# First feed-forward product as seven half-size products, its weight sums made in DRAM during the mixer

## The chip, the core and the metric

One core of a Trainium2 chip runs one launch of the kernel. The metric is the device time of that launch in microseconds; smaller is better. Engines work side by side, each in the order of its own instruction list: TensorE (PE) multiplies, VectorE (DVE) and ScalarE (ACT) do elementwise work, GpSimd (POOL) does some elementwise work and issues transfers, SyncE (SP) only issues transfers.

## The reference

One residual layer on x of 512 tokens and 1024 channels, in float32:

```python
D_MODEL = 1024; SEQ = 512; D_FF = 4 * D_MODEL
...
for l in range(DEPTH):
    h = rms_norm(x, norm_mix_pre[l])
...
    x = x + rms_norm(merged @ w_out[l], norm_mix_post[l])
    h = rms_norm(x, norm_ffn_pre[l])
    f = jnp.square(jax.nn.relu(h @ w_ff1[l])) @ w_ff2[l]
    x = x + rms_norm(f, norm_ffn_post[l])
```

The lines left out are the mixer: one input projection of h, cut into the parts of three branches (gated DeltaNet, stick-breaking attention, short gated convolution), whose outputs sigmoid gates merge. The part that changes is `h @ w_ff1`: 512 x 1024 by 1024 x 4096, and what feeds and follows it.

## The kernel before

All large products run on PE in float32r, each as three passes: both operands are split into a high and a low part, and high x high, high x low and low x high are summed in one bank (`mm3`, one instruction a pass through `mm`, L179). A weight tile (128 x 1024, 512 KB) is loaded by SP into `raw` (two buffers, `wload` L140), ACT casts it to the high part (L143), DVE subtracts to get the low part (L144); `hl` has three buffers. Every product is fed this way, so a weight tile costs one load, one ACT and one DVE instruction.

The Tile scheduler fixes each engine's order when the kernel is built; priorities (`early`, `urgent`) and the order of the code decide it. On the chip an engine takes its list strictly in order.

Stages: input projection and mixer (the `proj` calls, with the branches woven between them by lanes of generators), gates, out-projection (bank `po`), and for each of four blocks of 128 tokens a post-norm residual (`out_norm`: x1, then h2), transposes on PE (`out_transpose`, L898) and a split into `h2h` and `h2l`. Then ff1: 32 output tiles of 128 features, each 8 k-tiles x 3 passes of 512 columns (tokens); the first three tiles (`lead`) are done as two halves of 256 columns, the first half from token blocks 0 and 1 while blocks 2 and 3 are still being normalized. `ff1_act` takes relu on ACT (L942) and squares on DVE (L947) into the tiles `aT[i]`, i the half of the tokens.

ff2 is already done by seven products of half size in place of eight (Strassen's scheme in Winograd's form): the matrices are cut 2 x 2, and sums of blocks enter as operands. The sums of weight blocks it needs, S5, S6 and S1, are made in DRAM by `presum`: SP copies one block from DRAM to DRAM (L172), later POOL issues a transfer that adds the second block to it (L168). There are 24 such jobs; before, four are issued in the gate stage and twenty in ff1. POOL's elementwise work in the mixer is small but on the branches' path: `sv` and `DT` of each DeltaNet head (L456, L460), the masks of attention scores `z` (L651), the scratch transfers of a triangular inverse (`scr`, `tc`, L497 to L519) and the memset of `TT` (L525).

Of the kernel before, what the change touches and what calls it, by code (L numbers as in the profile page):

```python
# [62 lines left out]
def trunk_kernel(ctx, tc, keys, xT, xtok, wst, wab, cst, vec, alog, dtb, wpost, wffn, wfpost, out):  # L63
# [92 lines left out]
    for u in range(8):
        jobs.append((S5[u], ("ff2", 1, 8 + u), ("ff2", 1, u)))
    for u in range(8):
        jobs.append((S6[u], ("ff2", 0, u), ("ff2", 1, u)))
    for u in range(8):  # L160
        jobs.append((S1[u], S5[u], ("ff2", 0, u)))
# [762 lines left out]
    def ff1_mm(w, ps, ts_):  # L924
        wh = w[:, 0, :].rearrange("p (k c) -> p k c", k=KT)
        wl = w[:, 1, :].rearrange("p (k c) -> p k c", k=KT)
        for k in range(KT):
            mm3(ps[:, ts_], wh[:, k, :], wl[:, k, :], h2h[:, k, ts_], h2l[:, k, ts_], k == 0, k == KT - 1)

# [6 lines left out]
    def ff1_act(f, ps):  # L936
        u = f // 2
        if f % 2 == 0:
            for i in range(2):
                aT[i].append(g2("aT", F32, (P, 2, 256)))  # L940
        r = sm.tile([P, 512], F32, tag="r", bufs=2, name=nm("r"))
        x = nc.scalar.activation(r, ps, AF.Relu)  # L942
        if ready:
            dep(x, after[0])
        for i in range(2):
            c = slice(i * 256, i * 256 + 256)
            x = nc.vector.tensor_tensor(aT[i][u][:, f % 2, :], r[:, c], ps[:, c], ALU.mult)  # L947
            if ready:
                dep(x, after[1])
        if f % 2 == 1 and u >= 8:  # L950
            X.append(g2("X", F32, (P, 2, 256)))
            nc.vector.tensor_tensor(flat(X[-1]), flat(aT[0][u]), flat(aT[0][u - 8]), ALU.subtract)
            W.append(aT[0][u])
            nc.vector.tensor_tensor(flat(W[-1]), flat(W[-1]), flat(aT[1][u]), ALU.subtract)
# [2 lines left out]
    for i, (w, ps) in enumerate(lead):
        ff1_mm(w, ps, slice(0, 256))
        if i > 0:
            out_transpose(i + 1, h2s[i + 1])  # L960
    for f, (w, ps) in enumerate(lead):
        ff1_mm(w, ps, slice(256, 512))
        ff1_act(f, ps)
    NJ, NR = 4, 3
# [8 lines left out]
    def right(src, plus=None):  # L973
        if turn["r"] < NR:
            raw = ring("r", raws)
        else:
            if turn["r"] == NR:
                raws.clear()
                for _ in range(2):
                    t = hp.tile([P, 4, 1024], F32, tag="h16", name=nm("ch"))  # L980
                    raws.extend([(slice(0, 1024), t[:, i, :])] for i in range(4))
            raw = ring("r", raws)
# [31 lines left out]
    for f in range(3, 30):  # L1014
        if f >= 6:
            presum()
        w = wnext("ff1", f)
        ps = mbank()
        ff1_mm(w, ps, slice(0, 512))
        ff1_act(f, ps)  # L1020
    late = [(wnext("ff1", 30), mbank())]
    ff1_mm(*late[0], slice(0, 512))
    late.append((wnext("ff1", 31), mbank()))
    ready.append(unit(A10, block(0, 0), 0))
    ff1_act(30, late[0][1])
    ff1_mm(*late[1], slice(0, 512))
    ready.append(unit(A10, block(0, 0), 1))
    ff1_act(31, late[1][1])
# [168 lines left out]
```

## Time and profile before

| what | value |
|---|---|
| time of the kernel before, median of 3 runs | 908.04 us (906.22 to 908.98) |
| profiled execution, its own time | 908.15 us |
| its span in the trace | 906.4 us |
| PE busy | 884.8 us (98%) |
| DVE, ACT, POOL busy | 588.5, 451.8, 106.4 us |
| mean granted clock of PE | 0.995 |
| ff1, the piece at 512 columns | 587.11 to 744.90 us |

The profile is of one execution. The span runs from the first to the last instruction of the core; the time of the execution is a little longer. Busy time of an engine is a sum over the whole span: a stage may be bound by another engine than the mean suggests.

### The profile page before, as it was taken

What the parts mean: (1) busy time and instruction counts of PE and PEld (TensorE: products, weight loads), DVE (VectorE), ACT (ScalarE), POOL (GpSimd) and SP (SyncE); (2) the same over time, 40 slices, a digit from 0 to 9 for tenths busy, and PEclk for the clock granted to TensorE, in tenths of its full rate; (3) what the DMA queues carried; (4) which work ended last, traced back from release to release, by engine and by line L of the source; (5) the groups of instructions that cost most, each with busy time, mean ns of one, the idle gap of its engine ahead of it and who ended that gap; (6) DMA issues with size and microseconds to landing.
All of it is one profiled execution on the core that took longest, in us unless ns stands there. A gap on an engine that the chain in (4) does not pass through costs nothing.

```text
span 906.4 us, 11714 instructions
## 1 busy us (share of the span) xinstructions
PE 884.8 (98%) x4204; PEld 735.0 (81%) x4204; DVE 588.5 (65%) x1022; ACT 451.8 (50%) x823; POOL 106.4 (12%) x165
## 2 busy tenths in 40 slices
PE   7999999999999999999999999999999999999996
PEld 6778888877877888888888878988888888888884
DVE  4786678987778659655565546533334459878885
ACT  7455875657787732232344333422223337566562
POOL 1003222010112120200000111011111000000020
PEclk9999999999999999999999999999999999999998
DMA  9322223231213134524243552299999339565792
GB/s 316 119 71 93 73 74 122 70 106 51 68 57 104 51 125 116 163 94 116 70 151 119 180 190 94 86 298 284 278 286 274 125 117 364 189 198 193 202 270 86
DMA packets 41627, 136.97 MB, mean 151 GB/s; under 512 B 5456, under 2 KB 5456, under 8 KB 41184
## 3 DMA queue, kind: packets, MB, share of 16 engines
q1 hardware_dynamic: 34176, 111.50, 35.1%
q0 software_dynamic: 7248, 24.68, 13.1%
q8 instruction: 33, 0.54, 0.2%
q14 instruction: 26, 0.21, 0.1%
q10 hardware_dynamic: 144, 0.04, 0.0%
HBM read 131.48 MB, written 29.88 MB: 178 GB/s over the span
## 4 chain that ended last, share of the span: by engine, by line
PE 81%; DVE 10%; ACT 3%; issue 3%; DMA 2%; POOL 0%; DVEq 0%; SPq 0%; POOLq 0%; ACTq 0%
PE mm L179 51%; PE Q L179 5%; PE R L179 5%; PE S L179 5%; PE po L179 3%; PE psv L179 3%; PE V L179 2%; DVE hl L144 2%; DVE c L682 2%; PE p L179 2%; DMA raw<-wst 1%; DVE z L683 1%; DVE XX L513 1%; PE pg L179 1%; DVE XX L507 1%
## 5 line engine op out<-in xcount | busy, mean ns | idle before, releaser
L179 PE MATMUL mm<-hh,hl 128*128 128x512 f32 x928 | 305.8, 397 | 0.9 <-ACT ct L729 0.9
L143 ACT CAST hl<-raw 128x1024 fp32r<-128x1024 f32 x116 | 111.6, 962 | 222.3 <-PE mm L179 154.3
L144 DVE TENSOR_TENSOR hl<-raw,hl 128x1024 fp32r<-128x1024 f32 x116 | 129.0, 1112 | 142.5 <-ACT hl L143 142.2
L179 PEld LDWEIGHTS mm<-hh,hl 128*128 128x128 f32 x928 | 173.9, 188 | 35.7 <-ACT ct L729 1.3
L179 PE MATMUL mm<-hl,hl 128*128 128x512 f32 x464 | 181.2, 390 | 0.0
L179 PE MATMUL mm<-h2h,hl 128*128 128x512 f32 (+1 forms) x528 | 155.2, 377 | 0.4 <-ACT h2h L187 0.2
L179 PEld LDWEIGHTS mm<-h2h,hl 128*128 128x128 f32 x528 | 97.2, 188 | 19.0 <-ACT h2h L187 0.8
L179 PEld LDWEIGHTS mm<-hl,hl 128*128 128x128 f32 x464 | 87.4, 188 | 16.1
L179 PE MATMUL mm<-h2l,hl 128*128 128x512 f32 (+1 forms) x264 | 99.5, 377 | 0.1
L997 DVE TENSOR_TENSOR hl<-ch,hl 128x1024 fp32r<-128x1024 f32 x53 | 64.7, 1223 | 6.2 <-ACT hl L996 6.1
L179 PEld LDWEIGHTS mm<-h2l,hl 128*128 128x128 f32 x264 | 49.7, 188 | 9.3 <-DVE h2l L188 0.3
L996 ACT CAST hl<-ch 128x1024 fp32r<-128x1024 f32 x53 | 55.3, 1046 | 0.0
L179 PE MATMUL po<-wo,mg 128*128 128x512 f32 x192 | 45.3, 391 | 0.5 <-ACT mg L187 0.5
L179 PEld LDWEIGHTS po<-wo,mg 128*128 128x128 f32 x192 | 35.8, 188 | 8.5 <-ACT mg L187 1.0
L179 PE MATMUL Q<-hl,ahi 128*128 128x512 f32 x128 | 39.7, 391 | 0.0
L179 PE MATMUL R<-hl,ahi 128*128 128x512 f32 x128 | 39.4, 389 | 0.0
L179 PE MATMUL S<-hl,ahi 128*128 128x512 f32 x128 | 39.4, 389 | 0.0
L168 POOL DMA_DIRECT2D S<-wst x24 | 19.9, 830 | 152.0 <-DMA S<-wst 115.1
L682 DVE TENSOR_TENSOR_SCAN c<-c,w 128x512 f32<-128x512 f32 (+3 forms) x32 | 25.5, 816 | 14.9 <-ACT w L106 14.9
L187 ACT CAST ahi<-aT 128x512 fp32r<-128x512 f32 x32 | 19.8, 622 | 28.7 <-PE Q L179 12.1
L179 PEld LDWEIGHTS Q<-hl,ahi 128*128 128x128 f32 x128 | 23.9, 188 | 5.7 <-ACT hl L996 0.4
L947 DVE TENSOR_TENSOR aT<-r,mm 128x256 f32<-128x256 f32 x62 | 23.1, 415 | 7.7 <-ACT r L942 7.7
(287 smaller groups left out, 1442.0 us busy)
## 6 DMA issues: line engine op xcount, KB each, us to landing
raw<-wst SPq DMA_DIRECT2D x92, 512.0 KB, 3.3
ch<-S SPq DMA_DIRECT2D x32, 512.0 KB, 3.3
raw<-wst SPq DMA_DIRECT2D x48, 256.0 KB, 3.3
S<-wst POOLq DMA_DIRECT2D x24, 512.0 KB, 9.1
ch<-wst SPq DMA_DIRECT2D x21, 512.0 KB, 5.1
S<-wst SPq DMA_DIRECT2D x16, 512.0 KB, 8.1
S<-S SPq DMA_DIRECT2D x8, 512.0 KB, 9.7
ch<-wst POOLq DMA_DIRECT2D x8, 512.0 KB, 8.4
```

The costliest lines, as they stand in the source:

```text
L143: nc.scalar.copy(hl[:, 0, :], raw)
L144: nc.vector.tensor_tensor(hl[:, 1, :], raw, rf(hl[:, 0, :]), ALU.subtract)
L168: nc.gpsimd.dma_start(t, wsrc(1024, *key), accum_op=ALU.add, max_dma_last_dim=4096)
L179: return nc.tensor.matmul(o, l, r, start=start, stop=stop, skip_group_check=more)
L187: nc.scalar.copy(hi, src)
L507: nc.vector.tensor_tensor(tmp[:, :, :w], X[:, :, j].unsqueeze(2).to_broadcast([P, 8, w]), L[:, j, j + 1:].unsqueeze(1).to_broadcast([P, 8, ...
L513: nc.vector.tensor_tensor(X[:, :, j + 1:], X[:, :, j + 1:], tmp[:, :, :w], ALU.subtract)
L682: nc.vector.tensor_tensor_scan(back, back, w[j][:, ks][:, ::-1], 0.0, ALU.add, ALU.add)
L683: nc.vector.tensor_tensor(z[j][:, :n], z[j][:, :n], c[j][:, :n], ALU.subtract)
L947: x = nc.vector.tensor_tensor(aT[i][u][:, f % 2, :], r[:, c], ps[:, c], ALU.mult)
L996: after[0] = nc.scalar.copy(hl[0][:, c], r)
L997: after[1] = nc.vector.tensor_tensor(hl[1][:, c], r, rf(hl[0][:, c]), ALU.subtract)
```

## The change

ff1 becomes seven products too. The token half i and the feature half n give blocks: A of the activations (A00, A01, A10, A11: token half, channel half) and four blocks of w_ff1. With X, Y, Z, W as sums of activation blocks and F1, F5, F6, F7 as sums of weight blocks, M1 to M7 are seven products of 256 tokens x 512 channels x 2048 features in place of eight. Each product is cut into eight steps u of 256 features: two output tiles of 128 features lie side by side in one bank of 512 columns, and each takes 4 k-tiles x 3 passes = 12 matmuls of 256 columns, so 24 for a step. M5 is summed into M3's bank, M4 into M2's and M7 into M1's. `step` recombines the banks on DVE and takes relu and square; M3's bank is copied out by ACT. `combine` makes X, Y, Z and W on DVE from float32 copies `F` of the transposes, made by ACT, and splits each. F1, F5, F6 and F7 are 32 more `presum` jobs; these are issued from the third `proj` call on, `quiet` keeping some stretches of the triangular inverse free, and from every fourth product of ff1. The store of x1 goes from SP's to POOL's queue. Weights of ff1 go through a ring of five load buffers (the two `raw`, and three pairs of `rw`).

```diff
+    F5, F6, F1, F7 = (sums("F", n) for n in (5, 6, 1, 7))
+    plan(F5, f1(1, 1), f1(0, 1))
+    plan(F6, f1(0, 0), f1(0, 1))
+    plan(F1, F5, f1(0, 0))
+    plan(F7, F1, f1(1, 0))
...
     def presum():
+        if quiet[0]:
+            return
         while added and (len(added) > LAG or not jobs):
...
     def proj(c0, x=False):
+        calls[0] += 1
+        if calls[0] > 2:
+            presum()
         w = wnext("in", c0)
...
-            nc.sync.dma_start(x1d[b, hf], x1[hf])
+            nc.gpsimd.dma_start(x1d[b, hf], x1[hf])
...
-            split(h2h[:, q * 4:q * 4 + 4, bs], h2l[:, q * 4:q * 4 + 4, bs], p3)
+            if b % 2 == 0:
+                FB[i, q] = [g2("F", F32, (P, 2, 256)) for _ in range(2)]
+            for g in range(2):
+                nc.scalar.copy(FB[i, q][g][:, :, ts_], p3[:, 2 * g:2 * g + 2, :])
...
+        if i == 0:
+            combine(("A", 0, 0), FB[0, 0])
+            FB["X"] = [g2("X", F32, (P, 2, 256)) for _ in range(2)]
+            combine("X", FB["X"], FB[0, 1], FB[0, 0])
+        else:
+            combine(("A", 1, 0), FB[1, 0])
+            combine(("A", 1, 1), FB[1, 1])
+            combine("Y", FB["X"], FB[1, 1], FB["X"])
+            combine("Z", FB[1, 0], FB[1, 0], FB["X"])
+            combine("W", FB[0, 1], FB[0, 1], FB[1, 1])
+
+    def combine(name, o, a=None, b=None):
+        if name not in op:
+            op[name] = [[g2("op", F32R, (P, 2, 256)) for _ in range(2)] for _ in range(2)]
+        for g in range(2):
+            if a is not None:
+                nc.vector.tensor_tensor(o[g], a[g], b[g], ALU.subtract)
+            split(op[name][0][g], op[name][1][g], o[g])
...
-    lead = [(wnext("ff1", f), mbank()) for f in range(2)] + [(wnext("ff1", 2), bank("f1"))]
...
+    left = {"M1": "Y", "M2": ("A", 1, 0), "M3": "X", "M4": ("A", 1, 1), "M5": ("A", 0, 0), "M6": "Z", "M7": "W"}
...
+    def ff1_product(m, ps, u, first):
+        done[0] += 1
+        if done[0] > 5 and done[0] % 4 == 0:
             presum()
...
+        hi, lo = op[left[m]]
+        for j in range(2):
+            o = ps[:, j * 256:j * 256 + 256]
+            for k in range(4):
+                c = slice(k * 256 + j * P, k * 256 + j * P + P)
+                xh_, xl_ = hi[k // 2][:, k % 2, :], lo[k // 2][:, k % 2, :]
+                mm(o, w[0][:, c], xh_, first and j == 0 and k == 0, False, True)
+                mm(o, w[0][:, c], xl_, False, False, True)
+                mm(o, w[1][:, c], xh_, False, k == 3, True)
...
+        if m == "M3":
+            pb["R", u] = mbank()
+            ff1_product(m, pb["R", u], u, True)
+            nc.scalar.copy(new(1, 8 + u), pb["R", u])
...
+        elif m == "M5":
+            ff1_product(m, pb["R", u], u, False)
+            relu2(new(0, 8 + u), pb["R", u])
...
+    quiet[0] = False
+    step("M3", 0)
+    step("M3", 1)
+    out_transpose(2, h2s[2])
+    step("M5", 0)
+    out_transpose(3, h2s[3])
+    step("M5", 1)
+    for m in ("M2", "M4", "M1", "M6", "M7"):
+        step(m, 0)
+        if m in ("M2", "M4"):
+            step(m, 1)
+    for m in ("M1", "M6", "M7"):
+        step(m, 1)
+    for u in range(2, 8):
+        for m in ("M3", "M2", "M5", "M4", "M1", "M6", "M7"):
+            step(m, u)
```

How the order of instructions moves, at three places. A row is a line, an operation, its output and inputs with buffer numbers, and the output's shape; x23 is 23 such in a row.

The first place is PE behind the out-projection, at the start of ff1. Before, `pt` are transposes of blocks, `mm` and `f` the banks of the lead's tiles, whose halves begin between the transposes of block 2:

```order
L898 MATMUL pt_5188<-cs,h_953_5080 128x128 x4
L898 MATMUL pt_5195<-cs,h_954_5081 128x128 x4
L898 MATMUL pt_5268<-cs,h_960_5125 128x128 x3
L179 MATMUL mm_5207<-h2h,hl_5203 128x256
L179 MATMUL mm_5213<-h2h,hl_5209 128x256
L898 MATMUL pt_5268<-cs,h_960_5125 128x128
L898 MATMUL pt_5275<-cs,h_961_5126 128x128 x4
L179 MATMUL f_981_5219<-h2h,hl_5215 128x256
```

In the changed kernel `pt_5312` and `pt_5319` are of block 1, the next two of block 2 and the last two of block 3; `h_921` holds the split X and A00, `h_922` the split A10 and A11, `mm_5346` and `mm_5378` are the banks of M3 and M5 for u = 0 and 1, `Q` those of M2 and M4:

```order
L928 MATMUL pt_5312<-cs,h_961_5200 128x128 x4
L928 MATMUL pt_5319<-cs,h_962_5201 128x128 x4
L928 MATMUL pt_5410<-cs,h_968_5245 128x128 x4
L928 MATMUL pt_5419<-cs,h_969_5246 128x128 x4
L928 MATMUL pt_5463<-cs,h_981_5308 128x128 x4
L928 MATMUL pt_5470<-cs,h_982_5309 128x128 x4
L197 MATMUL mm_5346<-h_921_4973,hl_5349 128x256
L197 MATMUL mm_5378<-h_921_4973,hl_5381 128x256
L197 MATMUL mm_5346<-h_921_4973,hl_5349 128x256 x23
L197 MATMUL mm_5378<-h_921_4973,hl_5381 128x256 x23
L197 MATMUL mm_5346<-h_921_4973,hl_5430 128x256 x24
L197 MATMUL mm_5378<-h_921_4973,hl_5517 128x256 x24
```

The first product of ff1 now stands behind the transposes of the last block, where it stood between those of block 2.

The second place is ACT at the same time. Before, the casts of the last transposes (`h2h`), the weight casts and the relus of the lead follow each other:

```order
L861 ACTIVATE r_5175,st<-x_946_5035 128x512
L861 ACTIVATE r_5179,st<-x_947_5037 128x512
L187 CAST h2h<-pt_5306 128x4x128
L187 CAST h2h<-pt_5313 128x4x128
L143 CAST hl_5423<-raw_5422 128x1024
L942 ACTIVATE r_5346<-mm_5207 128x512
L143 CAST hl_5457<-raw_5456 128x1024
```

In the changed kernel `aT` are the copies of M3's banks, `F` those of the transposes of blocks 2 and 3, `hl_5430` the weights of M5 u = 0:

```order
L1088 COPY aT_5376<-mm_5346 128x512
L1088 COPY aT_5408<-mm_5378 128x512
L933 COPY F_5415<-pt_5410 128x2x128
L933 COPY F_5416<-pt_5410 128x2x128
L933 COPY F_5424<-pt_5419 128x2x128
L933 COPY F_5425<-pt_5419 128x2x128
L933 COPY F_5415<-pt_5463 128x2x128
L933 COPY F_5416<-pt_5463 128x2x128
L933 COPY F_5424<-pt_5470 128x2x128
L933 COPY F_5425<-pt_5470 128x2x128
L205 CAST h_922_4974<-F_5415 128x512
L205 CAST h_922_4974<-F_5416 128x512
```

and right behind them, with the relu of M5 u = 0 (`r_5460`), the casts of Y, Z and W (`op`) and the weights of M5 u = 1 (`hl_5517`):

```order
L205 CAST h_922_4974<-F_5424 128x512
L1025 CAST hl_5430<-rw_5100 128x512
L1025 CAST hl_5430<-rw_5101 128x512
L205 CAST h_922_4974<-F_5425 128x512
L1072 ACTIVATE r_5460<-mm_5346 128x512
L205 CAST op_5485<-X_5330 128x512
L205 CAST op_5486<-X_5331 128x512
L205 CAST op_5495<-F_5415 128x512
L205 CAST op_5496<-F_5416 128x512
L205 CAST op_5505<-F_5263 128x512
L205 CAST op_5506<-F_5264 128x512
L1025 CAST hl_5517<-rw_5102 128x512
```

The weights of M5 now stand behind the copies of M3's banks, the copies of the transposes and the operand casts.

The third place is POOL in the mixer, between the transfers of two DeltaNet heads (`scr`). Before:

```order
L497 DMA scr_1295<-AD_1009 128x4x32
L456 TENSOR_TENSOR sv_1106<-ske_1105,half 128x4
L460 TENSOR_TENSOR DT_765<-DT_765,wd_1107 128x512
L651 AFFINE_SELECT z_1190<-z_1190 128x128
L651 AFFINE_SELECT z_1191<-z_1191 128x256
L651 AFFINE_SELECT z_1192<-z_1192 128x128
```

In the changed kernel, where `F` are the weight sums in DRAM:

```order
L519 DMA scr_1350<-AD_1058 128x4x32
L186 DMA F_85<-wst 128x1024
L477 TENSOR_TENSOR sv_1157<-ske_1156,half 128x4
L481 TENSOR_TENSOR DT_806<-DT_806,wd_1158 128x512
L186 DMA F_86<-wst 128x1024
L676 AFFINE_SELECT z_1243<-z_1243 128x128
L676 AFFINE_SELECT z_1244<-z_1244 128x256
L676 AFFINE_SELECT z_1245<-z_1245 128x128
```

Two accumulating transfers have come in, one ahead of the head's `sv` and one ahead of the masks.

## Rows read from the trace of the kernel before

**Rows 1.** The page, busy time, share of the span and instructions of each engine.

```profile
PE 884.8 (98%) x4204; PEld 735.0 (81%) x4204; DVE 588.5 (65%) x1022; ACT 451.8 (50%) x823; POOL 106.4 (12%) x165
```

**Rows 2.** Chain of waits, out-projection to ff1: start us, us, what.

```profile
560.33 5.51 PE po L179 x24
...
584.35 2.76 PE f L179 x23
587.11 157.79 PE mm L179 x696
```

**Rows 3.** Windows: length; busy us of PE, PEld, DVE, ACT, POOL; granted clock, DMA share, GB/s.

```profile
251.83:255.25 3.42, 3.42 (x16) 3.33 (x15) 3.36 (x7) 2.58 (x8) 0.00 (x0) 0.50 0.10 17
300.00:456.00 156.00, 155.79 (x799) 130.95 (x798) 98.08 (x240) 56.90 (x134) 20.16 (x27) 1.00 0.37 108
587.11:744.90 157.79, 157.79 (x698) 130.64 (x697) 65.39 (x106) 46.02 (x62) 19.62 (x26) 1.00 0.82 236
600.00:690.00 90.00, 90.00 (x399) 74.53 (x398) 33.82 (x55) 24.73 (x32) 12.95 (x16) 1.00 1.02 287
```

**Rows 4.** Timeline at the start of ff1: start us, us, engine, instruction, idle before.

```profile
568.17 1.42 DVE L884 SCALAR_TENSOR_TENSOR x<-y,st,x 128x512 f32<-128x512 f32 x2
570.98 0.54 POOL L850 TENSOR_TENSOR st<-st,half 128x1 f32<-128x1 f32 x1 [2.85 <-DVE st L849]
571.56 1.42 DVE L890 SCALAR_TENSOR_TENSOR h<-x,st,wff 128x512 f32<-128x512 f32 x2
...
577.21 1.07 ACT L187 CAST h2h<-pt 128x512 fp32r<-128x512 f32 x2 [6.81 <-PE pt L898]
```

**Rows 5.** Groups in 587 to 745: instruction and count, busy us, mean ns.

```profile
L144 DVE TENSOR_TENSOR hl<-raw,hl 128x1024 fp32r<-128x1024 f32 x27 | 33.1, 1225 | 84.7 <-ACT hl L143 84.7
L143 ACT CAST hl<-raw 128x1024 fp32r<-128x1024 f32 x27 | 28.4, 1053 | 101.2 <-PE mm L179 58.1 <-DMA raw<-wst 43.1
...
L952 DVE TENSOR_TENSOR X<-aT,aT 128x512 f32<-128x512 f32 x7 | 4.8, 685 | 0.0
...
L996 ACT CAST hl<-rw 128x512 fp32r<-128x512 f32 x4 | 2.3, 622 | 0.0
```

**Rows 6.** Groups on ACT in 30 to 456: the narrowest copy.

```profile
L670 ACT COPY z<-z 128x256 f32<-128x256 f32 x8 | 3.1, 390 | 0.0
```

**Rows 7.** Transfers in 600 to 690: queues, then issues and us to landing.

```profile
q0 software_dynamic: 2307, 8.40, 52.5%
q1 hardware_dynamic: 2907, 17.40, 49.3%
...
raw<-wst SPq DMA_DIRECT2D x17, 512.0 KB, 8.2
S<-wst POOLq DMA_DIRECT2D x16, 512.0 KB, 9.3
S<-wst SPq DMA_DIRECT2D x8, 512.0 KB, 9.1
S<-S SPq DMA_DIRECT2D x8, 512.0 KB, 9.7
```

**Rows 8.** Timeline of PE in the mixer, its longest idle there.

```profile
251.19 0.71 PE L179 MATMUL p<-ct,AQ 128*128 128x128 f32 x4 [1.83 <-DVE S L596]
```

**Rows 9.** Timeline of POOL and of SP's queue in the mixer.

```profile
118.56 1.04 POOL L456 TENSOR_TENSOR sv<-ske,half 128x4 f32<-128x4 f32 x1 [7.38 <-DVE ske L455]
...
282.70 0.94 POOL L168 DMA_DIRECT2D S<-wst  x1 [1.89 <-DMA S<-wst]
...
340.92 0.90 POOL L168 DMA_DIRECT2D S<-wst  x1 [5.66 <-DMA S<-wst]
...
277.99 0.60 SPq L172 DMA_DIRECT2D S<-wst  x1
...
335.76 0.50 SPq L172 DMA_DIRECT2D S<-wst  x1
```

**Rows 10.** Waits of DVE in 33 to 456: total us, times, longest.

```profile
DVE wD L462 <- POOL DT L460: 5.8, 4, 1.8
```

More of the change, by code (lines that the diff above doesn't have):

```diff
@@ L150, in wsrc, with sums, plan, f1 @@
         return wst[keys.index(key)][:, :n]
-    S5, S6, S1 = ([dp.tile([P, 1024], F32, tag=f"{n}{u}", bufs=1, name=f"{n}{u}") for u in range(8)]
-                  for n in ("S5", "S6", "S1"))
+    def sums(which, n):
+        return [dp.tile([P, 1024], F32, tag=f"{which}{n}{u}", bufs=1, name=f"{which}{n}{u}") for u in range(8)]
     jobs = []
[L156 to L161, printed above, removed]
+    def plan(t, of, plus):
+        jobs.extend((t[u], of[u] if isinstance(of, list) else of(u), plus(u)) for u in range(8))
+    def f1(k, n):
+        return lambda u: ("ff1", k, n, u)
+    def f2(k, n):
+        return lambda u: ("ff2", n, 8 * k + u)
+    F5, F6, F1, F7 = (sums("F", n) for n in (5, 6, 1, 7))
[3 more added lines that the diff above has]
+    plan(F7, F1, f1(1, 0))
+    S5, S6, S1 = (sums("S", n) for n in (5, 6, 1))
+    plan(S5, f2(1, 1), f2(0, 1))
+    plan(S6, f2(0, 0), f2(0, 1))
+    plan(S1, S5, f2(0, 0))
+    quiet = [False]
+    calls = [0]
     added = []
@@ L820, in trunk_kernel @@
     mg, wo = [], []
+    quiet[0] = True
     def load_wo(u):
@@ L833, in trunk_kernel @@
         load_wo(dm)
+        quiet[0] = dm not in (0, 2, 4)
         a = gate_branch(dm, 0, ya)
@@ L851, in rs @@
         return st[:, b, col:col + 1]
-    h2h = hp.tile([P, KT, T], F32R, tag="h16", name="h2h")
-    h2l = hp.tile([P, KT, T], F32R, tag="h16", name="h2l")
+    FB, op = {}, {}
+    homes = [hp.tile([P, 4, 4, 256], F32R, tag="h16", name=nm("h2")) for _ in range(2)]
+    for j, (p_, q_) in enumerate(((("A", 0, 0), "X"), (("A", 1, 0), ("A", 1, 1)))):
+        op[p_] = [[homes[j][:, e, 2 * g:2 * g + 2, :] for g in range(2)] for e in range(2)]
+        op[q_] = [[homes[j][:, 2 + e, 2 * g:2 * g + 2, :] for g in range(2)] for e in range(2)]
     x1d = dp.tile([NB, 2, P, 512], F32, tag="x1d", bufs=1, name="x1d")
@@ L909, in trunk_kernel @@
         out_evac(po[b], b, 0)
+    NR = 3
+    raws = [[(slice(0, 512), g2("rw")), (slice(512, 1024), g2("rw"))] for _ in range(NR)]
     h2s = {}
@@ L920, in trunk_kernel @@
             out_transpose(b - 2, h2s[b - 2])
[L924 to L928, printed above, removed]
     aT = [[], []]
@@ L934, in trunk_kernel @@
     flat = lambda t: t.rearrange("p j c -> p (j c)")
[L936 to L954, printed above, removed]
-    lead = [(wnext("ff1", f), mbank()) for f in range(2)] + [(wnext("ff1", 2), bank("f1"))]
[L957 to L964, printed above, removed]
+    for i in range(2):
+        aT[i].extend([None] * 16)
+    NJ = 4
     stats = [(g2("ahi", F32R, (P, 2, 256)), g2("alo", F32R, (P, 2, 256))) for _ in range(NJ)]
-    raws = [[(slice(0, 512), g2("rw")), (slice(512, 1024), g2("rw"))] for _ in range(NR)]
     turn = {"s": 0, "r": 0, "w": 0}
@@ L971, in ring, with right @@
         return of[(turn[what] - 1) % len(of)]
-    def right(src, plus=None):
-        if turn["r"] < NR:
-            raw = ring("r", raws)
-        else:
[L977 to L982, printed above, removed]
+    both = (slice(0, 1024),)
+    def right(src, plus=None, second=True):
+        if second and turn["w"] == NR:
+            raws.clear()
+            for _ in range(2):
+                t = hp.tile([P, 4, 1024], F32, tag="h16", name=nm("ch"))
+                raws.extend([(both[0], t[:, i, :])] for i in range(4))
+        if not second and turn["r"] % (NR + 2) < 2:
+            turn["r"] += 1
+            raw = [(both[0], wp.tile([P, 1024], F32, tag="raw", bufs=2, name=nm("raw")))]
+        elif not second:
+            raw = raws[turn["r"] % (NR + 2) - 2]
+            turn["r"] += 1
+        else:
+            raw = raws[turn["w"] % len(raws)]
         for c, r in raw:
@@ L988, in right @@
                 nc.gpsimd.dma_start(r, plus[:, c], accum_op=ALU.add)
-        turn["w"] += 1
-        if turn["w"] % 4:
+        turn["w"] += second
+        if not second or turn["w"] % 4:
             hl = wp.tile([P, 2, 1024], F32R, tag="hl", bufs=3, name=nm("hl"))
@@ L1000, in block @@
     def block(k, n):
-        return lambda u: wsrc(1024, "ff2", n, 8 * k + u)
+        return lambda u: wsrc(1024, *f2(k, n)(u))
     def stat(t):
@@ L1013, in trunk_kernel @@
     A10 = lambda u: aT[1][u]
-    for f in range(3, 30):
-        if f >= 6:
-            presum()
[L1017 to L1028, printed above, removed]
+    wsum = {"M1": F1, "M5": F5, "M6": F6, "M7": F7, "M2": f1(0, 0), "M3": f1(1, 1), "M4": f1(1, 0)}
@@ new lines, in trunk_kernel @@
+    left = {"M1": "Y", "M2": ("A", 1, 0), "M3": "X", "M4": ("A", 1, 1), "M5": ("A", 0, 0), "M6": "Z", "M7": "W"}
+    done = [0]
+    def ff1_product(m, ps, u, first):
+        done[0] += 1
+        if done[0] > 5 and done[0] % 4 == 0:
+            presum()
+        b = wsum[m]
+        with early():
+            w = right(b[u] if isinstance(b, list) else wsrc(1024, *b(u)), None, False)
+        hi, lo = op[left[m]]
[7 more added lines that the diff above has]
+                mm(o, w[1][:, c], xh_, False, k == 3, True)
```

62 lines of the change are left out of this document (58 added, 4 removed).

## The prediction

> **What bounds the kernel now.** I read the page first: PE is busy for 98% of the span [rows 1], so a saving of PE work is a saving of time, if PE stays fed. The chain of waits then says where PE is released by others: around the first feed-forward product (ff1) the chain lies on PE from the end of the out-projection at 560.33 + 5.51 = 565.84 us, through a lead of 256-column halves, to one unbroken piece of 696 matmuls of 512 columns, 587.11 to 744.90 [rows 2]. A table of windows tells the same by stage: in 587.11 to 744.90 PE is busy all of it, DVE 65.39 us and ACT 46.02 us; in 300 to 456, in the mixer, PE is busy 155.79 of 156 us [rows 3]. So PE waits almost nowhere, and each new wait is a loss in full.
>
> **The saving.** 696 matmuls in 157.79 us are 226.7 ns each for 512 columns; the lead's 23 in 2.76 us are 120 ns each for 256 columns [rows 2]. ff1 before is 32 tiles x 8 k x 3 = 768 matmuls' worth: 696 x 0.2267 + 144 half-width x 0.120 = 157.8 + 17.3 = 175.1 us. After: 7 products x 8 u x 24 = 1344 matmuls of 256 columns, 161.3 us; one product is 24 x 0.120 = 2.88 us. **Saving: 13.8 us**. The half-width matmuls cost a little over half, so a part of the nominal eighth (21.9 us) is gone already. The Trainium skill ("TensorE: Matmul & The Clock Gate", Back-to-back issue gap) gives the isolated gap as columns / 2.4 GHz + 2.5 ns, that is 216 ns and 109 ns; by it the saving would be 768 x 216 - 1344 x 109 = 19 us, an estimate from that page. The rows are 5 and 10% above it, so they decide.
>
> **The start of ff1.** Before, the lead's tiles start on token blocks 0 and 1 while blocks 2 and 3 are still being normalized; weights were cast long ago. After, the order lists put all transposes ahead of the first product, and M3's operand X on DVE stands behind the last block's h2. I follow the chain on the old clock:
> - DVE's two h2 of block 3 start at 571.56 and end at 572.98 [rows 4]. X is two subtractions of 0.685 [rows 5], to 574.35; its two casts on ACT, 0.62 each [rows 5], and DVE's low halves let M3 run from about 575.0. The pair M3 u0, M3 u1 is 5.76 us: 580.7. PE idles from the last out-projection at 565.84 to 575, but for a few transposes.
> - ACT is in order: its copy of M3 u1's bank comes next, and behind that stand eight copies of the transposes of blocks 2 and 3 (256 elements each, 0.39 as the nearest row [rows 6]: 3.1 us), three casts and the two half casts of M5's weights (0.62 each: 3.1 us): 580.7 + 0.6 + 3.1 + 3.1 = 587.5; DVE's first low half allows M5 u0 at 587.3. It ends at 590.2. None of those copies needs M3; they wait behind an instruction that does.
> - ACT then has relu (0.6), six operand casts (Y, Z, W: 3.7) and the weights of M5 u1 (1.2): 595.7. M5 u1 runs 595.5 to 598.4. Relu and the weights of M2 u0 follow: PE starts M2 at about 600.1.
> - 52 products remain: 52 x 2.88 = 149.8, so ff1 ends at 749.9, against 744.90. **+5.0 us** net of the saving: PE's waits here eat 13.8 + 5.0 = 18.8 us. The bounds: +3.5 if a copy takes 0.33 and casts 0.59 (as h2h's two in 1.07 [rows 4], less overlap), +7 if each wait between engines adds 0.1 us a link.
> - Once blocks run, DVE has per u seven weight splits of 1.225 and twelve operations of 0.69 [rows 5]: 16.9 us, ACT 7 x 1.05 and five of 0.6: 10.4 us, under PE's 20.2. But for u = 0 and 1 ten products (28.8 us of PE) face ten splits and 22 operations, 27.5 us, with little slack for order: I take **+1.5** (0 to 3).
> - Transfers: in 600 to 690 before, 33 hardware-queue transfers (17 loads, 16 copies) took 49.3% and 16 accumulations 52.5% of the 16 DMA engines over 90 us [rows 7], so 1.34 and 2.95 us each. Four products take four loads, one copy, one accumulation: 9.7 us in 11.5. 84%, hidden behind a five-deep ring; before it ran at 1.02 [rows 3] and PE did not stop. Nothing added.
>
> **The clock.** Before, PE idled 1.83 us ahead of 251.19 [rows 8], and from 251.83 to 255.25 its granted clock was 0.50 [rows 3], that is 1.2 GHz in place of 2.4. The new start has three idle stretches of some 9 (with a few transposes), 6.6 and 5.3 us with one or two products between them. I expect half clock for some 3.4 us behind each, as in that row: M3 +1.7 to 2.2, M5 u0 and u1 up to 2.88 each but take 2.3, and M2 +1. **+8 us**; 0 if the clock holds, 12 if all of the start runs at half. The Trainium skill ("TensorE: Matmul & The Clock Gate", HAM oscillation) describes such a loss: an array that pauses between short bursts is throttled again and starts each burst cold. It speaks against this change; the row agrees with it.
>
> **The mixer.** By the order lists 28 sum jobs now run beside the in-projection, where four ran before from 278 us on. Each is a copy on SP's queue and an accumulation on POOL's, which waits for the copy: issued at 277.99 and 335.76, the accumulations ran at 282.70 and 340.92 after idling for the copy [rows 9]. So the copy holds POOL's in-order queue up to 4.7 to 5.2 us, and the issue takes 0.9 more. Behind such rows now stand sv and DT of a head (118.56 before [rows 9]), the z masks, the inverse's scratch transfers and TT. DVE already waited for DT four times, 5.8 us in all, the longest 1.8 [rows 10]; a later POOL reaches DVE, then PE through the recurrences. About nine places, each late by 1.5 us on average (0 if the copy is in, 5.7 if just issued), a third of it reaching PE, the rest under the 512-column products that fill PE there: **+4 us** (0 to 10, two places at full length). The weight loads share SP's queue with the copies, a few us later than before; they are issued well ahead and I add nothing. x1's store moves to POOL, two issues of 0.9 us at most [rows 9] between x1 (from 568.17, the last ready at 569.59) and the power at 570.98 [rows 4]: hidden, at worst +1. ff2 keeps its work: nothing.
>
> **Sum** against the profiled execution's 908.15 us (its span 906.4; the median of the runs is 908.04, so the same): 908.15 + 5.0 + 1.5 + 8 + 4 = 926.65. I predict 926.5 us, slower by 2%.
>
> **Rivals.**
> - *The clock holds, or the mixer hides its jobs* (either, 0.20): 914 to 919. For it: the old idle of 1.83 us is one case, and in the mixer's last third PE lost 0.2 of 156 us. Against: the new idles are three to five times that one.
> - *Faster, by a start that costs less* (0.09): if ACT's eight copies and the casts run while M3 does, M5 follows M3 at 580.7 and ff1 ends at 575.0 + 56 x 2.88 = 736.3, 8.6 us early: 899.5, or 903.5 with the mixer. For it: none of those copies needs M3's result. Against: ACT's list puts them behind the copy that waits for M3, and an engine takes its list in order. It decides when PE's waits between 565.84 and M2, clock included, stay under 13.8 us less the mixer's.
> - *The mixer dominates* (0.12): POOL's queue is held at six or more places for the full 5 us and the half of it reaches PE: +15 in place of +4, and with the start 937.
> - *Transfers bind ff1* (0.04): at 1.02 of the engines in place of 0.84 PE would wait a fifth of 150 us minus what the ring carries; 945 or more.
>
> **How the numbers follow.** The forecast itself (918 to 935) has 0.55. The measurement tells about 0.3%, 2.7 us, from no change. Faster by more is the second rival, 0.09; between it and the first lies 0.04 for the same; slower 0.87. The range 910 to 941 leaves out the second rival and the far end of the last two.
>
> **What would show it.** In the changed profile: 256-column matmuls 120 ns apart once u = 2 begins, a product 2.88 us; M3 first near 9 us after the last out-projection matmul; PE's longest idles ahead of M5 u0 and M5 u1, released by ACT or DVE at the weight cast; a granted clock of 0.5 in the 25 us after the out-projection; POOL idle for DMA ahead of sv and z, and the out-projection ending some 4 us later than 565.84. I am wrong if M5 runs on directly behind M3, or if the out-projection is not later, or ends more than 10 us later, or if DVE or a transfer releases PE again and again behind u = 2.

## The result and the profile after

The changed kernel takes 939.81 us (median of 4, 936.19 to 941.05) against 907.13 for the kernel before: ratio 1.0358 [1.0332, 1.0384], slower by 32.7 us. The forecast of 926.5 had the direction; the size came out beyond the 918 to 935 that it held likeliest and 1.2 us inside the far end of the whole range, 941.

The profiled execution took 936.19 us, its span 934.5. By stage, read from the end of the last matmul of the out-projection, the start of M2's first matmul and the start of ff2's first, where ff1 ends:

| us | before | changed | difference | forecast |
|---|---|---|---|---|
| end of the out-projection | 565.8 | 581.4 | +15.6 | +4 |
| from there to M2 u0 | - | 38.9 | | 34.3 + 8 |
| from the out-projection to the end of ff1 | 178.9 | 190.9 | +12.0 | +14.5 |
| ff2 and the rest | 161.7 | 162.2 | +0.5 | 0 |

The page of the changed kernel, busy time and granted clock by slices; they answer to [rows 1]: PE has 504 more matmul records than before and 2.5 us less busy time, in a span that is 28 us longer.

```profile
PE 882.3 (94%) x4708; PEld 757.1 (81%) x4708; DVE 655.9 (70%) x1109; ACT 491.7 (53%) x910; POOL 137.5 (15%) x205
...
PEclk9999999999999999999999999779999999999998
```

The timeline of PE at the start of ff1 answers to [rows 2, 4]. In brackets is the idle time ahead of a row and what ended it.

```profile
575.70 5.74 PE L197 MATMUL po<-wo,mg 128*128 128x512 f32 x24
...
588.71 1.94 PE L928 MATMUL pt<-cs,h 128*128 128x128 f32 x8 [4.93 <-DVE h L920]
590.53 7.97 PE L197 MATMUL mm<-h,hl 128*128 128x256 f32 x48
603.45 5.46 PE L197 MATMUL mm<-h,hl 128*128 128x256 f32 x24 [4.93 <-ACT hl L1025]
613.22 0.80 PE L197 MATMUL mm<-h,hl 128*128 128x256 f32 x2 [4.31 <-ACT hl L1025]
614.53 4.63 PE L197 MATMUL mm<-h,hl 128*128 128x256 f32 x22 [0.52 <-DVE hl L1026]
620.36 0.50 PE L197 MATMUL Q<-h,hl 128*128 128x256 f32 x2 [1.19 <-ACT hl L1025]
```

M3 begins 9.1 us behind the out-projection (forecast 9.2), and both M5 steps wait for ACT's cast of their weights. ACT's timeline shows why: the copies of the transposes (`F`), which need nothing of M3, stand behind the copies of M3's banks (`aT`), and the weights (`hl`) behind both.

```profile
595.79 0.59 ACT L1088 COPY aT<-mm 128x512 f32<-128x512 f32 x1 [4.71 <-PE mm L197]
598.55 0.58 ACT L1088 COPY aT<-mm 128x512 f32<-128x512 f32 x1 [2.17 <-PE mm L197]
599.03 2.31 ACT L933 COPY F<-pt 128x256 f32<-128x256 f32 x8
601.13 1.74 ACT L205 CAST h<-F 128x512 fp32r<-128x512 f32 x3
602.70 1.22 ACT L1025 CAST hl<-rw 128x512 fp32r<-128x512 f32 x2
...
610.47 2.18 ACT L205 CAST op<-F 128x512 fp32r<-128x512 f32 x4
612.54 1.14 ACT L1025 CAST hl<-rw 128x512 fp32r<-128x512 f32 x2
```

Windows of the changed kernel (columns as in [rows 3]): the granted clock is 0.50 in the first 4.1 us of M3 and in nearly all of both M5 steps. Later ff1 is all PE, and in the mixer PE is busy 404.30 of 423 us.

```profile
33.00:456.00 423.00, 404.30 (x2014) 336.37 (x2013) 298.49 (x610) 238.60 (x494) 89.10 (x126) 0.99 0.68 182
...
587.79:594.62 6.83, 5.91 (x25) 5.43 (x26) 3.91 (x6) 1.22 (x2) 0.93 (x1) 0.50 0.62 184
...
601.45:608.27 6.82, 4.81 (x21) 4.52 (x22) 6.82 (x12) 2.98 (x6) 0.00 (x0) 0.50 0.25 80
611.69:618.51 6.82, 4.78 (x20) 4.48 (x21) 3.39 (x6) 1.99 (x4) 0.00 (x0) 0.50 0.23 77
...
625.34:772.29 146.95, 146.95 (x1226) 146.95 (x1226) 121.11 (x174) 75.78 (x120) 8.51 (x11) 1.00 0.86 263
```

The same window of the mixer in the kernel before, which the rows ahead of the prediction did not show:

```profile
33.00:456.00 423.00, 416.09 (x2084) 347.02 (x2083) 306.51 (x624) 243.56 (x503) 61.31 (x91) 1.00 0.29 90
```

What POOL waited for in this stretch of the changed kernel (total us, times, longest), and a piece of its timeline that answers to [rows 9]: POOL stands 9.3 us at an accumulation, and `sv` and `DT` of a head run behind it. SP issued the copy that it stands for only at 118.22, 3.7 us after POOL had come to it.

```profile
POOL S L186 <- DMA S<-wst: 92.4, 10, 21.0
POOL F L186 <- DMA F<-F: 87.2, 14, 11.0
POOL F L186 <- DMA F<-wst: 69.5, 14, 11.3
```

```profile
118.22 0.50 SPq L190 DMA_DIRECT2D F<-wst  x1
...
123.81 0.89 POOL L186 DMA_DIRECT2D F<-wst  x1 [9.29 <-DMA F<-wst]
124.44 1.34 POOL L477 TENSOR_TENSOR sv<-ske,half 128x4 f32<-128x4 f32 x1
125.47 1.32 POOL L481 TENSOR_TENSOR DT<-DT,wd 128x512 f32<-128x512 f32 x1
```

DVE's waits on POOL's side in the same stretch answer to [rows 10]. In the changed kernel:

```profile
DVE wD L483 <- POOL DT L481: 12.1, 4, 4.5
DVE vs L638 <- POOL f L637: 6.1, 2, 4.0
DVE XX L531 <- DMA L<-scr: 4.6, 1, 4.6
DVE TT L554 <- POOL TT L550: 3.1, 1, 3.1
```

In the kernel before, beside the 5.8 us for `DT`:

```profile
DVE vs L613 <- POOL f L612: 5.7, 4, 1.8
```

So the theory to test: the loss has two causes that do not depend on each other. POOL's in-order queue stands at accumulations in the mixer, and the order of the lists at the start of ff1 leaves PE without work, which lowers its clock as well. Rivals: the added transfers themselves (weight loads late behind copies), the late sums as M5's weights, and the amount of work on ACT and DVE.

### The profile page after: what moved, and what is told of

It is laid out like the page before. It is cut to its first block, busy times and chain, and to the rows that moved or that the text cites. A ratio compares the mean times of both kernels' runs of the same rounds, so it can differ in the third digit from the quotient of the medians.

```text
span 934.5 us, 13188 instructions
## 1 busy us (share of the span) xinstructions
PE 882.3 (94%) x4708; PEld 757.1 (81%) x4708; DVE 655.9 (70%) x1109; ACT 491.7 (53%) x910; POOL 137.5 (15%) x205
## 4 chain that ended last, share of the span: by engine, by line
PE 62%; DVE 12%; DMA 9%; issue 8%; ACT 5%; POOL 3%; SPq 0%; POOLq 0%; DVEq 0%; ACTq 0%
PE mm L197 30%; PE Q L197 10%; PE V L197 5%; PE R L197 5%; PE S L197 4%; DVE hl L144 3%; PE psv L197 3%; DMA F<-F 2%; DMA F<-wst 2%; DMA raw<-wst 2%; PE p L197 1%; DVE c L707 1%; DVE XX L537 1%; DVE XX L531 1%; DMA S<-wst 1%
## 5 line engine op out<-in xcount | busy, mean ns | idle before, releaser
L143 ACT CAST hl<-raw 128x1024 fp32r<-128x1024 f32 x84 | 77.8, 926 | 105.0 <-PE mm L197 75.2
L144 DVE TENSOR_TENSOR hl<-raw,hl 128x1024 fp32r<-128x1024 f32 x84 | 89.6, 1068 | 46.8 <-ACT hl L143 46.7
L1025 ACT CAST hl<-rw 128x512 fp32r<-128x512 f32 x72 | 41.2, 620 | 46.8 <-issue 23.6
L197 PE MATMUL mm<-h,hl 128*128 128x256 f32 x384 | 55.4, 305 | 9.8 <-ACT hl L1025 9.2
L197 PEld LDWEIGHTS mm<-h,hl 128*128 128x128 f32 x384 | 52.9, 213 | 11.3 <-ACT hl L1025 9.7
L197 PE MATMUL Q<-h,hl 128*128 128x256 f32 x384 | 50.1, 289 | 1.5 <-ACT hl L1025 1.2
L1026 DVE TENSOR_TENSOR hl<-rw,hl 128x512 fp32r<-128x512 f32 x72 | 46.5, 687 | 5.9 <-ACT hl L1025 5.8
L197 PEld LDWEIGHTS Q<-h,hl 128*128 128x128 f32 x384 | 48.6, 198 | 1.9 <-ACT hl L1025 1.4
L197 PE MATMUL mm<-op,hl 128*128 128x256 f32 x384 | 48.5, 283 | 0.0
L197 PEld LDWEIGHTS mm<-op,hl 128*128 128x128 f32 x384 | 47.2, 192 | 0.0
```

The lines of the kernel that those rows point to most:

```text
L143: nc.scalar.copy(hl[:, 0, :], raw)
L144: nc.vector.tensor_tensor(hl[:, 1, :], raw, rf(hl[:, 0, :]), ALU.subtract)
L197: return nc.tensor.matmul(o, l, r, start=start, stop=stop, skip_group_check=more)
L1025: after[0] = nc.scalar.copy(hl[0][:, c], r)
L1026: after[1] = nc.vector.tensor_tensor(hl[1][:, c], r, rf(hl[0][:, c]), ALU.subtract)
```

## The experiments

Landmarks of all profiled executions, read as in the table above (us; M2 and ff1 counted from the out-projection's end):

| kernel | out-projection ends | M2 u0 | ff1 ends |
|---|---|---|---|
| before | 565.8 | - | +178.9 |
| changed | 581.4 | +38.9 | +190.9 |
| e1 sums in the mixer, old ff1 | 589.0 | - | +178.9 |
| e2 new ff1 only, sums dense | 564.7 | +37.7 | +196.6 |
| e10 new ff1 only, sums as in the change | 563.5 | +38.3 | +190.2 |
| e8 no accumulations before ff1 | 570.3 | +38.5 | +190.5 |
| e5 accumulations later | 572.5 | +37.1 | +189.0 |
| e7 dummy matmuls at the start | 587.9 | +35.5 | +185.9 |
| e4 other order at the start | 584.3 | +20.5 | +177.8 |
| e6 e4 and e5 together | 565.6 | +19.9 | +174.2 |
| e9 e6 with Z earlier | 567.9 | +20.4 | +175.2 |

**The two halves of the change alone (e1, e2, e10).** e1 is the kernel before with the change's 56 sum jobs and their schedule:

```diff
+    for n, c0, c1 in ((5, 0, 8), (6, 16, 8), (1, None, 16), (7, None, 24)):
+        for u in range(8):
+            of = ("ff1", c0 + u) if c0 is not None else FS[{1: 5, 7: 1}[n]][u]
+            jobs.append((FS[n][u], of, ("ff1", c1 + u)))
...
+        if calls[0] > 2:
+            presum()
```

> The kernel before with its own first feed-forward product (ff1), but with the change's 32 further sums and its schedule of sum jobs in the mixer and the gates; ff1 does not use the new sums. Theory (the sums in the mixer cost what the out-projection came later, 581.4 in place of 565.8 us): the out-projection ends near 581, ff1 and ff2 take what they took before, 907 + 15 = 922 us (919 to 925). Rival (the sums are hidden, and the later out-projection comes from the other order of the code or from x1's store on POOL): 907 to 910 us.

930.84 us, ratio 1.0263 [1.0218, 1.0308]. The mixer's cost stands alone: the out-projection ends 23.2 us late, and ff1 takes its 178.9 to the tenth. The time lies above the 919 to 925 expected, and executions of e1 spread from 925.3 to 933.3. What is larger than in the changed kernel is mostly not PE's wait but its clock: in the mixer PE is busy 403.86 us (404.30 there), but with 1981 matmuls in place of 2014, at a granted clock of 0.98:

```profile
33.00:456.00 423.00, 403.86 (x1981) 335.68 (x1980) 296.47 (x603) 237.09 (x489) 87.80 (x125) 0.98 0.67 179
```

The rival is out.

e2 is the changed kernel without F's jobs, so it leaves the sums of ff1's weights out:

```diff
-    wsum = {"M1": F1, "M5": F5, "M6": F6, "M7": F7, "M2": f1(0, 0), "M3": f1(1, 1), "M4": f1(1, 0)}
+    wsum = {"M1": f1(0, 1), "M5": f1(0, 1), "M6": f1(0, 0), "M7": f1(1, 0), "M2": f1(0, 0), "M3": f1(1, 1), "M4": f1(1, 0)}
...
-        if done[0] > 5 and done[0] % 4 == 0:
+        if done[0] > 5 and done[0] % 2 == 0:
             presum()
```

> The changed kernel without the 32 new sums: M1, M5, M6 and M7 take one plain block of w_ff1 as weights where the sum belongs (so the sums of weights are left out of the computation); the 24 old sums are issued four in the gates and the rest in ff1. Theory (parts add up): the out-projection ends near 566, and from there to the end of ff1 it takes 191 us as in the changed kernel: 907 + 12 = 919 us (916 to 922). Rival (the waits ahead of M5 come from the sums of weights, which are late in DRAM): the two idles ahead of M5 shrink, 905 to 913 us.

925.30 us, ratio 1.0210 [1.0181, 1.0240]: neither. The idles ahead of M5 are the same (M2 at 37.7), so the rival is out: M5 does not wait for the sums. But ff1 takes 5.8 us longer than in the changed kernel. The window of e2's later ff1 shows the transfer share at 0.95 and PE busy 131.33 of 136 us; ACT waited for loads of weights, fourteen times:

```profile
625.00:761.00 136.00, 131.33 (x1078) 130.68 (x1077) 104.91 (x152) 67.49 (x107) 13.08 (x17) 0.99 0.95 307
```

```profile
ACT hl L1021 <- DMA rw<-wst: 16.6, 6, 3.4
...
ACT hl L1021 <- DMA raw<-wst: 15.5, 8, 3.5
```

That is my own edit's doing: one sum job per two products in place of one per four. e10 has the change's rate (its edit against e2):

```diff
-    plan(S1, S5, f2(0, 0))
+    S1 = [wsrc(1024, *f2(0, 0)(u)) for u in range(8)]
...
-        if done[0] > 5 and done[0] % 2 == 0:
+        if done[0] > 5 and done[0] % 4 == 0:
```

> e2 again with the changed kernel's rate of sum jobs in ff1, one per four products (e2 had one per two): four S jobs in the gates, twelve in ff1; the eight S1 sums of ff2 are left out as well (a plain block stands in for each). Theory (new ff1 alone): the out-projection ends at 565 to 567 us, ff1 191 us behind that, 907 + 12 = 919 us, and e2's further 6 us were PE waiting for weights behind the denser sums. Rival (something else of the new ff1 is slower without the sums of the mixer): 925 us as e2.

919.49 us, ratio 1.0145 [1.0109, 1.0182], as expected: ff1 ends 190.2 us behind the out-projection, and its later part is all PE with a transfer share of 0.85:

```profile
610.00:753.00 143.00, 143.00 (x1194) 143.00 (x1193) 118.27 (x170) 74.50 (x118) 7.32 (x9) 1.00 0.85 263
```

e1's loss and e10's, 24.5 and 12.8 us, make 37 where the change lost 32.7: the parts add up as far as the mixer's own spread allows. The Trainium skill ("DMA: Bandwidth & Descriptors", Issuing engines are not separate DMA queues) says that transfers from different engines interleave on the same 16 DMA engines. The traces agree: in these windows a 256 KB load of weights on SP's queue took 11.4 us from issue to landing in e2, beside 16 accumulations of POOL, and 5.2 us in e10, beside 9. The share alone does not say when PE stops: before the change it was 1.02 in 600 to 690 [rows 3] and PE ran on, with a weight tile for 24 matmuls of 512 columns, 5.4 us, in place of 2.9.

**What in the mixer costs (e5, e8).** e5 keeps all transfers and adds an ordering edge, which makes nothing wait on the chip and only places the accumulation later in POOL's list:

```diff
+            wcast[0] = nc.scalar.copy(hl[:, 0, :], raw)
...
-            nc.gpsimd.dma_start(t, wsrc(1024, *key), accum_op=ALU.add, max_dma_last_dim=4096)
+            x = nc.gpsimd.dma_start(t, wsrc(1024, *key), accum_op=ALU.add, max_dma_last_dim=4096)
+            dep(x, wcast[0])
```

> The changed kernel with the accumulations of the mixer placed later in POOL's order, by an ordering edge to the cast of the weights loaded last; same transfers, same work. Theory (the mixer's 15.6 us come from POOL's queue standing at accumulations whose copy has not landed): most of the wait is gone and the out-projection ends 8 to 13 us earlier than in the changed kernel, 927 to 932 us. Rival (they come from the added transfers themselves, which make weight loads and scratch transfers late): out-projection as late as in the changed kernel, 937 to 941 us.

924.79 us, ratio 1.0200 [1.0163, 1.0236]: 15 us better than the changed kernel by the medians, more than expected; between the two profiled executions it is 10.8, of which the out-projection's end gives 8.9. Its window of the mixer has the change's transfers (share 0.66 against 0.68) and nearly the PE time of the kernel before, 413.95 of 423 us; `sv` no longer has an accumulation that waits ahead of it:

```profile
33.00:456.00 423.00, 413.95 (x2081) 344.75 (x2080) 306.14 (x623) 243.32 (x503) 92.24 (x129) 1.00 0.66 181
```

```profile
120.63 1.04 POOL L480 TENSOR_TENSOR sv<-ske,half 128x4 f32<-128x4 f32 x1 [7.35 <-DVE ske L479]
...
122.64 0.89 POOL L188 DMA_DIRECT2D F<-wst  x1
```

e8 leaves out the accumulations that the code issues before ff1; three of ff1's run early, at 440, 461 and 481 us:

```diff
-            nc.gpsimd.dma_start(t, wsrc(1024, *key), accum_op=ALU.add, max_dma_last_dim=4096)
+            if done[0]:
+                nc.gpsimd.dma_start(t, wsrc(1024, *key), accum_op=ALU.add, max_dma_last_dim=4096)
```

> The changed kernel without the accumulations before ff1: the copies of the sums' first blocks stay, the second blocks are not added (so the weight sums made in the mixer are left out). Theory (POOL's queue standing at accumulations is most of the mixer's loss, the rest are weight loads behind the copies): the out-projection ends 2 to 6 us later than before (565.8), 924 us. Rival (copies on SP's queue hold the weight loads): it ends 10 us later or more.

927.15 us (one execution, 3 above the 924 named), the out-projection 4.5 us late, within the theory's 2 to 6. But 2.6 us of it lie in the first 15 us, where PE is busy 7.75 us against 10.36 before; the first copy of a sum is issued only behind them, so the sums do not cause these. In 33 to 456 PE is as busy as before, though the copies on SP's queue are all there:

```profile
33.00:456.00 423.00, 416.05 (x2078) 346.62 (x2077) 304.15 (x621) 242.62 (x502) 58.27 (x88) 1.00 0.39 133
```

The rest of the delay, 1.6 us in e8 and 4.0 of e5's 6.7, arises behind 456 us, in the last gates (in 456 to 563 PE is busy 104.58 and 102.16 us, 106.15 before). A window there has PE busy 27.02 of 30 us in the changed kernel (first row), 25.88 in e5 (second), and in e6, which issues no sums beside these gates, 30.00, as before:

```profile
470.00:500.00 30.00, 27.02 (x118) 21.71 (x117) 14.83 (x21) 11.29 (x17) 1.68 (x2) 1.00 0.65 175
```

```profile
470.00:500.00 30.00, 25.88 (x105) 20.90 (x106) 14.01 (x21) 11.56 (x18) 0.81 (x1) 0.94 0.60 172
```

```profile
470.00:500.00 30.00, 30.00 (x134) 24.72 (x133) 17.28 (x25) 12.82 (x20) 0.00 (x0) 1.00 0.47 153
```

There the rival holds on a small scale: transfers of sums beside the loads for the gates and the out-projection. The changed kernel's trace shows such a wait. ACT stands for the load of a tile of the out-projection's weights (`wo`), which SP issued at 487.40, behind a copy at 486.86; the sigmoid (`sg`) that frees PE's bank follows at 493.11:

```profile
492.58 0.62 ACT L205 CAST wo<-raw 128x512 fp32r<-128x512 f32 x1 [4.95 <-DMA raw<-wst]
```

```profile
493.75 3.06 PE L197 MATMUL mm<-ya,hl 128*128 128x512 f32 x12 [1.65 <-ACT sg L106]
```

e6 differs from e5 in the start as well, so the size of this share is argued from the stage, not isolated.

**The start (e4, e7).** e4 has the same work in another order; its core (`ff1_weight` loads and casts a step's weights ahead of its matmuls):

```diff
+        if b == 3:
+            out_transpose(1, h2s[1])
         out_evac(ps, b, 1)
         h2s[b] = out_norm(b)
...
+    out_transpose(2, h2s[2])
+    ff1_weight("M3", 0)
+    ff1_weight("M3", 1)
+    ff1_weight("M5", 0)
...
     step("M3", 0)
     step("M3", 1)
-    out_transpose(2, h2s[2])
...
+    ff1_weight("M5", 1)
...
+    out_transpose(3, h2s[3])
     step("M5", 0)
-    out_transpose(3, h2s[3])
     step("M5", 1)
```

> The changed kernel with another order at the start of ff1 alone: X ahead of the last block's h2, the last block's transposes behind M3, M5's weights cast ahead of the copies of M3's banks and of the transposes, relu of M5 and the operands Y, Z, W behind the weights of M2. Same work. Theory (the waits of the start come from the order of ACT's and DVE's lists, and the low clock from these waits): M2 begins some 16 to 20 us behind the out-projection's end in place of 39, time 939.8 - 21 = 919 us (915 to 924). Rival (the start is bound by the amount of work on ACT and DVE, in whatever order): less than 8 us gained, 932 us or more.

921.57 us, ratio 1.0166 [1.0111, 1.0221]: 18 us gained by the medians, among them what the mixer varies (executions from 915.3 to 926.5). PE's timeline of e4: M3 4.4 us behind the out-projection, both M5 steps directly behind the last block's transposes, and M2 at +20.5:

```profile
588.72 0.80 PE L197 MATMUL mm<-h,hl 128*128 128x256 f32 x2 [2.07 <-ACT h L205]
...
598.15 1.03 PE L931 MATMUL pt<-cs,h 128*128 128x128 f32 x8
598.94 6.00 PE L197 MATMUL mm<-h,hl 128*128 128x256 f32 x48
604.77 5.92 PE L197 MATMUL Q<-h,hl 128*128 128x256 f32 x48
614.01 5.98 PE L197 MATMUL Q<-h,hl 128*128 128x256 f32 x48 [3.32 <-DVE aT L1095]
```

The work itself was no bound. A part of the gain goes again at 614.01: M4 adds to M2's bank and waits for DVE's subtraction (L1095, at 613.19), which stood behind the low halves of a weight (L1029, at 611.38) that needed a buffer of M2. ff1 ends 13.1 us earlier than in the changed kernel, not 18.4.

e7 leaves ACT's and DVE's lists as they are and fills two idles of PE:

```diff
+    def warm(n, behind):
+        ps = mbank()
+        for _ in range(n):
+            x = mm(ps[:, 0:P], cr, cr)
+            dep(x, behind)
+            behind = x
+        return x
...
+    end3 = last[0]
...
+    wm["M5"] = warm(60, end3)
     step("M5", 0)
     out_transpose(3, h2s[3])
+    wm["M5"] = warm(50, last[0])
     step("M5", 1)
```

> The changed kernel with 60 matmuls of 128 columns whose result nobody reads ahead of M5 u0 and 50 ahead of M5 u1, where PE idled 4.9 and 4.3 us; the lists of ACT and DVE are the same as in the changed kernel. Theory (the low clock comes from these idles): the granted clock stays at 1.0 through both M5 steps and M2, each M5 step takes 2.9 us in place of some 5, M2 begins 4 to 5 us earlier behind the out-projection's end (39 in the changed kernel): 935 us. Rival (the clock is not what lengthens these steps, they wait for weights and low halves): M2 as late as before, 938 to 941 us.

934.34 us, ratio 1.0297 [1.0266, 1.0328]. Timeline and a window of e7:

```profile
603.98 6.81 PE L197 MATMUL mm<-cr 128*128 128x128 f32 x60
610.63 3.09 PE L197 MATMUL mm<-h,hl 128*128 128x256 f32 x24
613.55 5.69 PE L197 MATMUL mm<-cr 128*128 128x128 f32 x50
619.09 3.14 PE L197 MATMUL mm<-h,hl 128*128 128x256 f32 x24
```

```profile
599.16:640.00 40.84, 39.33 (x333) 38.92 (x332) 27.70 (x43) 21.26 (x40) 0.82 (x1) 1.00 0.50 145
```

The M5 steps take 3.1 us in place of 5.5, at a granted clock of 1.00, though the dummies overran both idles by more than a microsecond. M2 begins 3.4 us earlier (4 to 5 expected) and ff1 ends 4.9 us earlier, counted from the out-projection; the total shows about as much, on a mixer that took longer in the profiled execution. So at the M5 steps the clock's loss is real and comes from the idles; M3's idle was left as it was.

**Both together (e6, e9).** e6 adds to e4 and e5:

```diff
-        quiet[0] = dm not in (0, 2, 4)
+        quiet[0] = True
...
-        if done[0] > 5 and done[0] % 4 == 0:
+        if done[0] > 5 and done[0] % 3 == 0:
...
+    castdep.append(sub2[0])
+    ff1_weight("M1", 0)
+    castdep.clear()
```

> The later accumulations of e5 and the order at the start of e4 in one kernel; also M2's subtraction ahead of M1's weight casts on DVE (e4 lost 3.3 us there), no sums issued beside the last gates, and one sum per three products in ff1 in place of four. Theory (the two causes are separate and their gains add): the out-projection ends 4 to 7 us later than before, ff1 ends some 173 to 177 us behind it (178.8 before): 904 to 911 us. Rival (transfers bind as soon as PE no longer waits): PE waits for weights in ff1, 913 us or more.

903.07 us (12 executions), ratio 0.9969 [0.9957, 0.9981]: 37 us below the changed kernel. Against the kernel before it gains 0.3%: the interval leaves out 1, but single executions of either kernel differ by more. The out-projection ends no later than before (565.6; I had expected 4 to 7 us), and ff1 is 4.7 us shorter than before. M2 on PE, and the window of later ff1:

```profile
585.48 12.01 PE L200 MATMUL Q<-h,hl 128*128 128x256 f32 x96
```

```profile
606.38:739.78 133.40, 133.40 (x1113) 133.31 (x1112) 110.10 (x160) 69.15 (x110) 8.47 (x11) 1.00 0.86 267
```

A denser job rate than the change's, one per three products, did not hold PE up.

e9 makes Z ahead of the relu of M4 (its edit against e6):

```diff
     combine("Y", FB["X"], FB[1, 1], FB["X"])
+    combine("Z", FB[1, 0], FB[1, 0], FB["X"])
+    castz = lastc[0]
     step("M4", 0)
     step("M4", 1)
...
-    combine("Z", FB[1, 0], FB[1, 0], FB["X"])
```

> e6 with one thing moved: Z is made ahead of the relu of M4, so that M6 u0 can follow M1 u0 directly; in e6 M1 u1 came between and PE idled 1.2 and 0.9 us there, with a short piece at half clock behind. Theory: ff1 ends about 171 us behind the out-projection's end in place of 174.2, 900 us. Rival (DVE is then the bound of this stretch, the wait moves to the next product): 903 us, as e6.

904.53 us, ratio 0.9980 [0.9969, 0.9992]: no gain over e6. M6 now follows M1, but ff1 ends no earlier (+175.2). The rival holds: PE waits for later products (1.2 us the longest), and in e6 DVE was busy 20.81 of the 20.90 us from 585.5 to 606.4.

## Why the prediction was right, and where its size was off

- **The saving** held: 52 products from M2's first matmul took 772.29 - 620.36 = 151.9 us against 149.8, a matmul of 256 columns 120 ns. The difference is about the low clock's last piece; the +1.5 us for DVE's load on u = 0 and 1 did not show, and behind 625 us PE never waits.
- **The start** was right in mechanism and nearly in size: M3 9.1 us behind the out-projection (9.2), idles of 4.9 and 4.3 us (6.6 and 5.3), all released by ACT's weight casts. The copies were the largest mis-sized piece: eight in 2.31 us, 0.29 each, where I took 0.39 from the row of `z`; PE also began on the first half of the cast weights and did not wait for the low half, as I had it.
- **The clock** was right: M3 7.97 us in place of 5.76, the M5 steps 5.5 and 5.4 in place of 2.88, and M2's first products: about 9 us against 8. PE worked 4.1 us of M3 and 4.8 of each M5 step at half clock, where I took 3.4 behind each idle. The Trainium skill ("TensorE: Matmul & The Clock Gate", HAM oscillation) describes this throttling between bursts, and the trace agrees (0.50 in the three windows above).
- **The transfers** in ff1 were right: share 0.86 (0.84 worked out). My reason, that PE had run on at 1.02, was weak: at 0.95 e2 lost 5.8 us.
- **The mixer** is the term that was mis-sized: +4 taken (0 to 10), 15.6 measured in the profiled execution, 23.2 in e1. By the prediction's own sign (the out-projection more than 10 us later) it was wrong here, and the size is that of the third rival, which I gave 0.12. That the whole stayed in the range is luck: the start came out 2.5 us cheaper than forecast, without which it would have passed 941.

Two steps of the mixer's term failed. The first is that a third of the delay would reach PE, because PE rarely waited before. At DVE the delay came out as forecast: nine places of 1.5 us are 13.5 us, and DVE's waits in the rows above rose from 5.8 + 5.7 = 11.5 us to 25.9, by 14.4. But PE's busy time in the window fell from 416.09 to 404.30 us, by 11.8, which is some four fifths of that and not a third. e5, without most of the stands, has 413.95. These are sums; the single chains were not followed. The granted clock fell as well, to 0.99 in this window and 0.98 in e1, from 1.00 before; I had no term for that. The second step is the weight loads behind the copies, to which I added nothing: PE lost 3.0 us in 470 to 500, where the loads of `wo` came late.

The count and the bound beneath were off too. I counted 28 jobs; 41 accumulations ran in 33 to 456 us, and POOL stood for a transfer at 38 of them, 249 us in all against 46 before. I also took a stand to last no longer than its copy, 5.7 us at most. It can last longer, as POOL may come to the accumulation before SP has issued the copy: so it was at 18 of the 38, with copies and accumulations paired in order, and the longest stand was 21.0 us. The kernel before had such a row already, which I did not use: the accumulation at 415.46 us had stood 36.09 us for a copy issued at 410.52.

That PE never waited for a chain did not say that the chain had slack. One sum among the rivals is also wrong: a mixer that hides its jobs alone gives 926.65 - 4 = 922.65 us, not 914 to 919.

## What to carry to other kernels

A transfer that waits, on an engine that also computes in order, costs what stands behind it; place it where its input has long landed, or on a queue with nothing else. A full engine in the old profile gives no measure of slack in the chains that feed it. When a product is cut finer, look at the static order of the first steps: an engine's copy of one result can hold the operands of the next, and each idle is paid twice where the clock falls, as it did here ahead of both M5 steps.
